# Sums of weight blocks in a seven-product scheme: formed by accumulating transfers instead of VectorE additions

## The chip, the cores and the metric

The kernel runs on one core of a Trainium2 chip. The metric is the device time of one execution in microseconds. Before the change, three runs gave 1434.34 us in the median (1432.75 to 1437.7).

The engines are called as the profile calls them: PE is the matrix engine (PEld its weight loads), DVE the vector engine, ACT the scalar engine, POOL the GpSimd engine and SP the sync engine, which here only issues transfers. A "transfer" is a DMA. SP, ACT and POOL each have a queue of their own in which their instructions, transfers included, are started in order.

## The reference

One decoder layer for a prompt of 1024 rows and 8 sample rows, all in float32 (`NT` = 1032 columns when the activations are stored transposed). After a normalisation, one projection `h @ w_in` (1024 to about 10,000 columns) feeds two branches; the change touches the weights of branch A's projection and of branch B's output projection:

```
proj = h @ w_in
hA, cA, bA, zA, qkv, zB, beta_raw, alpha_raw, gA, gB = jnp.split(proj, offs, axis=-1)
a_conv, new_buf_a = causal_dwconv(cA * hA, buf_a, conv_a_w)
yA = ((bA * a_conv) * jax.nn.silu(zA)) @ w_out_a
...                       # branch B: gated delta rule, o
yB = o.reshape(bsz, L, D_V).astype(x.dtype) @ w_out_b
merged = jax.nn.sigmoid(gA) * yA + jax.nn.sigmoid(gB) * yB
post = rmsnorm(merged @ w_o, norm_post)
```

Eight outputs are returned (both groups' rows and six new states). Only the products named above matter here.

## The kernel before, in words

**Precision.** Every large product is made of three matmuls of a reduced-precision type: an operand is split into a high part (`hi`, a rounding copy) and a low part (`lo`, the operand minus `hi`), and hi*hi, hi*lo and lo*hi are added in PSUM. So each block of weights costs one cast on ACT (`whi`) and one subtraction on DVE (`wlo`) before PE can use it.

**Stages.** A start, then a long run of ordinary projections (`run(jobs, 1, isp)`), then `products()`, `products_b()`, the output projection of branch A and the tail. The change lies in `products()` and `products_b()`.

**Seven products for eight.** There, output and operands are cut in two by two blocks and a Winograd form of Strassen's scheme is used: seven block products, called `P1, P2, P6, P7, P4, P5, P3` in the order of work. `products()` does this for five groups of column tiles (`t` = 3 to 7, called groups 3 to 7 below), `products_b()` for branch B's output projection with two halves `g` per product (group B). One product of one group is a *unit*: 48 matmuls of 258 columns. The weights of a group are four raw blocks of 128 x 1024 floats, `a11`, `a12`, `a21`, `a22` (keys `(group, odd, half, g)`), and the products use these: P1 a11; P2 a12; P6 a21 + a22 - a11; P7 a11 - a21; P4 a22; P5 a21 + a22 (`wsum`); P3 a12 - (a21 + a22 - a11). `evacuate` adds each product from PSUM to the output tiles (`acc`, or `mrg` in group B) on DVE; P1 is copied by ACT.

**How weights are prepared.** `weight_load` issues the raw blocks on SP's queue, two transfers of 256 KB a block. `weight_gen` waits until the unit before has begun (`unit[0] >= n - 1`), casts `whi` on ACT and subtracts `wlo` on DVE. The tiles `whi` and `wlo` have two buffers each, so the cast for a unit also waits until PE has finished the unit before the last. When P2's weights are split, four DVE additions of 128 x 1024 form the sums in place: `wsum`, then a21 (for P7), a11 (for P6) and a12 (for P3).

**What sets the order.** The generators (`weight_gen`, `park_gen`, `yblock_gen` and so on) are strands that a planner (`Sched`, `slot`, `force`) steps between groups of matmuls by assumed costs. The layer below places the recorded instructions into each engine's queue and may move them ahead of others; so the order in a queue is not that of the code, and it is shown below where it matters. Each engine works its queue in order: an instruction that waits holds up all behind it. Slots for raw blocks come from a common pool (`T4`).

**Other work in the same stretch.** `finish_group` closes a group on ACT and DVE, `park_gen` transforms the right operand of group B and stores it (`txs`), and `yblock_gen` loads it back: from `yBsc` on SP (`yraw`) for P1, P2, P3 and from `txs` on POOL's queue (`thi`, `tlo`) for the others. These 16 loads are all that POOL's queue issues before the change in these stages.

Lines: all calls go through one recording helper, so the profile has line L121 for nearly everything and the tiles' names tell the place: `wr` is a raw block, `wsum` the sum for P5, `pm_t` and `pa_t` are PSUM tiles.

Of the kernel before, what the change touches and what calls it, by code (L numbers as in the profile page):

```python
# [11 lines left out]
AF = mybir.ActivationFunctionType  # L12
ALU = mybir.AluOpType
# [3 lines left out]
P = 128  # L17
D = 1024
# [135 lines left out]
def hybrid_step(  # L154
# [9 lines left out]
    V, A, PE, GP, SY = (Paced(e, n, sched) for e, n in (  # L164
        (nc.vector, "V"), (nc.scalar, "A"), (nc.tensor, "PE"), (nc.gpsimd, "GP"), (nc.sync, "SY")))
# [12 lines left out]
    def tt(out, a, b, op):  # L178
        V.tensor_tensor(out=out, in0=a, in1=b, op=op)
# [15 lines left out]
    def act(out, in_, func, **kw):  # L195
        A.activation(out=out, in_=in_, func=func, **kw)
# [468 lines left out]
    def when(*conds):  # L665
        while not all(c() for c in conds):
            yield
# [710 lines left out]
    ACOL = (COL_H, COL_C, COL_B, COL_Z)  # L1378

    def alloc(key, side):  # L1380
        pools[key] = tc.alloc_tile_pool(name=key, bufs=1, side=side)
        return pools[key]

    UNITS = [(t, p, 0) for t in range(SG, NK) for p in PROD] + [("B", p, g) for p in PROD for g in range(2)]

    def weight_load(raw):
        for key in list(range(SG, NK)) + ["B"]:
            w, n = (w_out_b, 2) if key == "B" else (w_in, 1)
            for odd, half in ((0, 0), (0, 1), (1, 0), (1, 1)):
                for g in range(n):  # L1390
                    yield from when(lambda: len(raw) < 4 * n, lambda: T4.ready())
                    v = T4.get("wr", D)
                    for q in range(2):
                        c0 = (4 * g + 2 * q + odd) * P if n == 2 else ACOL[2 * q + odd] + key * P
                        SY.dma_start(out=v[:, q * 512:(q + 1) * 512].rearrange("p (k c) -> p k c", c=P),
                                     in_=w[0, half * 512:(half + 1) * 512, c0:c0 + P]
                                     .rearrange("(k p) c -> p k c", p=P))
                    raw[key, odd, half, g] = v
                    yield

    def weight_gen(raw):

        sums = {}
        for n, (key, p, g) in enumerate(UNITS):
            a11, a12, a21, a22 = ((key, o, hf, g) for o in range(2) for hf in range(2))
            src = {"P1": a11, "P2": a12, "P6": a11, "P7": a21, "P4": a22, "P5": None, "P3": a12}[p]
            yield from when(lambda: unit[0] >= n - 1, lambda: src is None or src in raw)
            hi_ = wpool.tile([P, NK, P], F32R, tag="whi", name="whi", bufs=2)
            lo_ = wpool.tile([P, NK, P], F32R, tag="wlo", name="wlo", bufs=2)
            hi, lo = (v.rearrange("p k c -> p (k c)") for v in (hi_, lo_))  # L1410
            v = raw[src] if src else sums.pop(g)
            A.copy(out=hi, in_=v)
            yield
            tt(lo, v, hi.bitcast(F32), ALU.subtract)
            made[key, p, g] = (hi_, lo_)
            yield
            if p == "P2":
                yield from when(lambda: a22 in raw and a21 in raw)
                s_ = wpool.tile([P, NK, P], F32, tag="wraw", name="wsum", bufs=3)
                s_ = sums[g] = s_.rearrange("p k c -> p (k c)")  # L1420
                tt(s_, raw[a21], raw[a22], ALU.add)
                yield
                tt(raw[a21], raw[a11], raw[a21], ALU.subtract)
                tt(raw[a11], s_, raw[a11], ALU.subtract)
                yield
                tt(raw[a12], raw[a12], raw[a11], ALU.subtract)
            elif p in ("P6", "P7", "P4", "P3"):
                T4.give(raw.pop(src))

    def park_gen():  # L1430

        for k in range(4):
            yield from when(lambda: T4.ready(2))
            a, b = T4.get("pa_", NT), T4.get("pb_", NT)
            SY.dma_start(out=a, in_=yBsc[k])
            SY.dma_start(out=b, in_=yBsc[4 + k])
            yield
            a1, a2, b1, b2 = a[:, 0:HT], a[:, HT:NT], b[:, 0:HT], b[:, HT:NT]
            tt(a1, a2, a1, ALU.subtract)
            tt(a2, b2, a2, ALU.subtract)  # L1440
            yield
            tt(b2, b2, a1, ALU.subtract)
            tt(b1, b1, b2, ALU.subtract)
            yield
            for r, v in enumerate((a, b)):
                yield from when(lambda: T4.ready(2))
                hi, lo = T4.get("phi", NT), T4.get("plo", NT)
                A.copy(out=hi.bitcast(F32R), in_=v)
                yield
                tt(lo.bitcast(F32R), v, hi, ALU.subtract)  # L1450
                T4.give(v)
                store(txs[r, 0, k].bitcast(F32), hi)
                store(txs[r, 1, k].bitcast(F32), lo)
                T4.give(hi)
                T4.give(lo)
                yield
        parked.append(True)
# [146 lines left out]
    def evacuate(p, v, ta, tb, half):  # L1604
        c1, c2 = (slice(o + half * PW, o + half * PW + PW) for o in (0, HT))
        C11, C12, C21, C22 = ta[:, c1], ta[:, c2], tb[:, c1], tb[:, c2]
        if p == "P1":
            A.copy(out=C11, in_=v)
            A.copy(out=C12, in_=v)
        for out, in_ in {"P1": (), "P2": ((C11, C11),), "P6": ((C12, C12),), "P7": ((C22, C12),),  # L1610
                         "P4": ((C21, C22),), "P5": ((C22, C22), (C12, C12)), "P3": ((C12, C12),)}[p]:
            tt(out, v, in_, ALU.add)

    gated = {}

# [52 lines left out]
    def to_products():  # L1668
        drain_bg()
        bp.release()  # L1670
        T4.extend(alloc("m", "left"), "sl", NSL, NT)
        raw = {}
        for g in (weight_load(raw), weight_gen(raw), block_gen()):
            start(g)
# [77 lines left out]
    T4 = Slots(alloc("t4", "left"), "t4", NT4, CY)  # L1752
# [64 lines left out]
    for j in range(9):  # L1817
        i, n, xr, mh, ml, held = pre.pop(j)
# [33 lines left out]
        for half in range(2):  # L1852
            hs = slice(half * 512, (half + 1) * 512)
            stt(yt[:n, hs], yt[:n, hs], r, xr[:n, hs], ALU.mult, ALU.add)
            out = y_prompt[0, i * P:(i + 1) * P, hs] if i < 8 else y_sample[:, 0, hs]
# [38 lines left out]
```

## Time and profile before

| | before |
|---|---|
| median of 3 runs | 1434.34 us |
| the profiled execution | 1434.01 us, span 1432.3 us |
| PE busy | 1401.0 us (98%) |
| DVE busy | 984.4 us (69%) |
| ACT busy | 656.4 us (46%) |
| POOL busy | 35.6 us (2%) |
| bytes moved by transfers | 158.59 MB, of these 8.46 MB from POOL's queue |
| granted PE clock | 0.998 |

The span runs from the first to the last instruction; the execution's own time is 1.7 us more. Matmuls are pipelined, so PE's busy time overlaps itself: one matmul of 258 columns has a mean of 282 ns in the records, but they start 120 ns apart. Times inside the span are given in us from its start. Group 3 begins at about 941, group 7's first product at 1103.33, group B at about 1143.6, and the seven-product stages end at about 1225.

### The profile page before, as it was taken

To read this page: it belongs to the slowest core of one execution; us is meant where nothing else is said; L and a number is where in the kernel's file an instruction comes from. 1 tells how busy PE (TensorE), PEld (TensorE's weight loads), DVE (VectorE), ACT (ScalarE), POOL (GpSimd) and SP (SyncE) were. 2 spreads that over 40 slices of the span, in tenths; PEclk is the share of its full clock that TensorE was granted. 3 is DMA by queue.
4 is the path that set the end of the run, shared out by engine and by line. 5 is a ranking of instruction groups with operands and counts; after the bars stand their busy time and mean duration, and the time that the engine had idled before them with its cause. 6 is when DMAs were issued, how large, how long until landed. Compare 5 with 4: busy or idle time off the path is not lost.

```text
span 1432.3 us, 25802 instructions
## 1 busy us (share of the span) xinstructions
PE 1401.0 (98%) x10130; PEld 1340.5 (94%) x10130; DVE 984.4 (69%) x2436; ACT 656.4 (46%) x1521; POOL 35.6 (2%) x59
## 2 busy tenths in 40 slices
PE   6999999899999999999999999999999999999997
PEld 4899999899999999999999999999999999999786
DVE  6754867759569585496864924988877867854553
ACT  6766453855528554466383332253323344532211
POOL 0000000100001000000000000000000110000000
PEclk9999999999999999999999999999999999999999
DMA  9523143132422324224132221344711885743221
GB/s 320 144 48 102 54 127 81 54 80 78 119 60 69 94 62 117 50 66 121 54 97 68 79 68 32 118 170 164 243 53 42 236 265 172 244 150 91 92 87 59
DMA packets 181922, 158.59 MB, mean 111 GB/s; under 512 B 25351, under 2 KB 157856, under 8 KB 181794
## 3 DMA queue, kind: packets, MB, share of 16 engines
q1 hardware_dynamic: 177248, 148.43, 35.2%
q0 software_dynamic: 4352, 8.46, 2.0%
q8 instruction: 79, 1.29, 0.4%
q14 instruction: 41, 0.34, 0.1%
q10 hardware_dynamic: 202, 0.08, 0.0%
HBM read 120.25 MB, written 36.91 MB: 110 GB/s over the span
## 4 chain that ended last, share of the span: by engine, by line
PE 84%; DVE 8%; DMA 5%; ACT 1%; issue 1%; SPq 1%; DVEq 0%; ACTq 0%
PE pm_t L121 63%; PE pa_t L121 19%; PE pb L121 2%; DVE acc L121 2%; DVE wlo L121 1%; DMA xs<-in_x_prompt_dram 1%; SPq L121 1%; DMA yraw<-yAsc 1%; DVE Tt L121 1%; DVE kq L121 1%; DMA wor<-in_w_o_dram 1%; DVE Ttmp L121 1%; DVE wr L121 0%; DMA yraw<-yBsc 0%; DMA pa__11678<-yBsc 0%
## 5 line engine op out<-in xcount | busy, mean ns | idle before, releaser
L121 PE MATMUL pm_t<-xh,whi 128*128 128x344 f32 (+1 forms) x1576 | 517.9, 329 | 2.2 <-ACT gate L121 2.2
L121 PE MATMUL pm_t<-xh,wlo 128*128 128x344 f32 (+1 forms) x1576 | 500.4, 318 | 0.0
L121 PE MATMUL pm_t<-xl,whi 128*128 128x344 f32 (+1 forms) x1576 | 500.1, 317 | 0.0
L121 PEld LDWEIGHTS pm_t<-xh,whi 128*128 128x128 f32 x1576 | 297.4, 189 | 4.7 <-ACT gate L121 2.5
L121 PEld LDWEIGHTS pm_t<-xl,whi 128*128 128x128 f32 x1576 | 297.3, 189 | 0.2
L121 PEld LDWEIGHTS pm_t<-xh,wlo 128*128 128x128 f32 x1576 | 296.9, 188 | 0.4
L121 DVE TENSOR_TENSOR wlo<-wraw,whi 128x512 fp32r<-128x512 f32 x136 | 91.8, 684 | 65.2 <-ACT whi L121 63.1
L121 ACT CAST whi<-wraw 128x512 fp32r<-128x512 f32 x136 | 82.7, 623 | 85.6 <-PE pm_t L121 83.6
L121 DVE TENSOR_TENSOR Ttmp<-Tt 32x30 f32<-32x30 f32 (+14 forms) x240 | 76.1, 317 | 14.7 <-DMA Tt<-sA 10.3
L121 DVE TENSOR_TENSOR Tt<-Tt,Ttmp 32x30 f32<-32x30 f32 (+14 forms) x240 | 76.2, 317 | 4.4
L121 ACT CAST whi<-wr 128x1024 fp32r<-128x1024 f32 x42 | 44.0, 1047 | 73.5 <-PE pa_t L121 34.9
L121 DVE SCALAR_TENSOR_TENSOR kq<-raw,vecs,kq 128x528 f32<-128x528 f32 x96 | 69.9, 758 | 1.5 <-ACT kq L121 1.3
L121 PE MATMUL pm_t<-thi,wlo 128*128 128x258 f32 x240 | 67.6, 283 | 1.6 <-DVE wlo L121 1.6
L121 PE MATMUL pm_t<-tlo,whi 128*128 128x258 f32 x240 | 67.6, 282 | 0.0
L121 PE MATMUL pm_t<-thi,whi 128*128 128x258 f32 x240 | 67.6, 282 | 0.0
L121 PE MATMUL pa_t<-thi,whi 128*128 128x258 f32 x224 | 63.3, 282 | 1.1 <-ACT whi L121 1.1
L121 PE MATMUL pa_t<-thi,wlo 128*128 128x258 f32 x224 | 63.4, 283 | 0.8 <-DVE wlo L121 0.8
L121 PE MATMUL pa_t<-tlo,whi 128*128 128x258 f32 x224 | 63.2, 282 | 0.0
L121 PE MATMUL pm_t<-yhi,whi 128*128 128x344 f32 x192 | 61.5, 321 | 0.0
L121 PE MATMUL pm_t<-ylo,whi 128*128 128x344 f32 x192 | 61.4, 321 | 0.0
L121 PE MATMUL pm_t<-yhi,wlo 128*128 128x344 f32 x192 | 61.4, 320 | 0.0
L121 DVE TENSOR_TENSOR wlo<-wr,whi 128x1024 fp32r<-128x1024 f32 x42 | 51.3, 1221 | 8.9 <-ACT whi L121 8.7
(406 smaller groups left out, 2834.0 us busy)
## 6 DMA issues: line engine op xcount, KB each, us to landing
wraw<-in_w_in_dram SPq DMA_DIRECT2D x60, 512.0 KB
wr<-in_w_in_dram SPq DMA_DIRECT2D x40, 256.0 KB
aw<-in_ada_w_dram SPq DMA_DIRECT2D x16, 512.0 KB
gBsc<-gate SPq DMA_DIRECT2D x8, 516.0 KB
gAsc<-gate SPq DMA_DIRECT2D x8, 516.0 KB
txs<-phi SPq DMA_DIRECT2D x8, 516.0 KB
txs<-plo SPq DMA_DIRECT2D x8, 516.0 KB
tlo<-txs POOLq DMA_DIRECT2D x8, 516.0 KB, 7.3
```

What stands on the lines that cost most here:

```text
L121: r = f(*args, **kw)
```

## The change

The four DVE additions of each group (and each half of group B) go. Transfers that add to what lies in the destination take their place; they are issued on POOL's queue (`GP.dma_start(..., accum_op=ALU.add)`), and their sign comes from ACT, which writes the negative of a block.

After P1's split: ACT writes -a11 into a new slot (the later a21) and then negates a11 in place. Then a21 and a22 are read from DRAM again and added to the slot of a11 (giving a21 + a22 - a11 for P6), and a21 is added to the new slot (a21 - a11 for P7). After P2's split: ACT negates a12 in place, a transfer inside SBUF adds a11's slot to it (for P3, with the sign turned), and `wsum` is loaded with a22 from SP's queue and a21 added to it. The block a21 is no longer loaded as such. P7 and P3 now have the opposite sign, so `evacuate` subtracts them.

```diff
--- before.py
+++ after.py
@@ -1383,18 +1383,27 @@
 
     UNITS = [(t, p, 0) for t in range(SG, NK) for p in PROD] + [("B", p, g) for p in PROD for g in range(2)]
 
+    def wd(v, key, add=False):
+
+        t, odd, half, g = key
+        w, n = (w_out_b, 2) if t == "B" else (w_in, 1)
+        for q in range(2):
+            c0 = (4 * g + 2 * q + odd) * P if n == 2 else ACOL[2 * q + odd] + t * P
+            out = v[:, q * 512:(q + 1) * 512].rearrange("p (k c) -> p k c", c=P)
+            in_ = w[0, half * 512:(half + 1) * 512, c0:c0 + P].rearrange("(k p) c -> p k c", p=P)
+            if add:
+                GP.dma_start(out=out, in_=in_, accum_op=ALU.add)
+            else:
+                SY.dma_start(out=out, in_=in_)
+
     def weight_load(raw):
         for key in list(range(SG, NK)) + ["B"]:
-            w, n = (w_out_b, 2) if key == "B" else (w_in, 1)
-            for odd, half in ((0, 0), (0, 1), (1, 0), (1, 1)):
+            n = 2 if key == "B" else 1
+            for odd, half in ((0, 0), (0, 1), (1, 1)):
                 for g in range(n):
                     yield from when(lambda: len(raw) < 4 * n, lambda: T4.ready())
                     v = T4.get("wr", D)
-                    for q in range(2):
-                        c0 = (4 * g + 2 * q + odd) * P if n == 2 else ACOL[2 * q + odd] + key * P
-                        SY.dma_start(out=v[:, q * 512:(q + 1) * 512].rearrange("p (k c) -> p k c", c=P),
-                                     in_=w[0, half * 512:(half + 1) * 512, c0:c0 + P]
-                                     .rearrange("(k p) c -> p k c", p=P))
+                    wd(v, (key, odd, half, g))
                     raw[key, odd, half, g] = v
                     yield
 
@@ -1414,18 +1423,26 @@
             tt(lo, v, hi.bitcast(F32), ALU.subtract)
             made[key, p, g] = (hi_, lo_)
             yield
-            if p == "P2":
-                yield from when(lambda: a22 in raw and a21 in raw)
+            if p == "P1":
+
+                yield from when(lambda: T4.ready())
+                raw[a21] = T4.get("wr", D)
+                act(raw[a21], raw[a11], AF.Copy, scale=-1.0)
+                act(raw[a11], raw[a11], AF.Copy, scale=-1.0)
+                wd(raw[a11], a21, True)
+                wd(raw[a11], a22, True)
+                wd(raw[a21], a21, True)
+            elif p == "P2":
+
+                act(raw[a12], raw[a12], AF.Copy, scale=-1.0)
+                GP.dma_start(out=raw[a12], in_=raw[a11], accum_op=ALU.add)
                 s_ = wpool.tile([P, NK, P], F32, tag="wraw", name="wsum", bufs=3)
                 s_ = sums[g] = s_.rearrange("p k c -> p (k c)")
-                tt(s_, raw[a21], raw[a22], ALU.add)
-                yield
-                tt(raw[a21], raw[a11], raw[a21], ALU.subtract)
-                tt(raw[a11], s_, raw[a11], ALU.subtract)
-                yield
-                tt(raw[a12], raw[a12], raw[a11], ALU.subtract)
-            elif p in ("P6", "P7", "P4", "P3"):
+                wd(s_, a22)
+                wd(s_, a21, True)
+            if p in ("P6", "P7", "P4", "P3"):
                 T4.give(raw.pop(src))
+            yield
 
     def park_gen():
 
@@ -1609,7 +1626,10 @@
             A.copy(out=C12, in_=v)
         for out, in_ in {"P1": (), "P2": ((C11, C11),), "P6": ((C12, C12),), "P7": ((C22, C12),),
                          "P4": ((C21, C22),), "P5": ((C22, C22), (C12, C12)), "P3": ((C12, C12),)}[p]:
-            tt(out, v, in_, ALU.add)
+            if p in ("P7", "P3"):
+                tt(out, in_, v, ALU.subtract)
+            else:
+                tt(out, v, in_, ALU.add)
 
     gated = {}
```

For one group this makes, before: 8 transfers of 256 KB from SP. After: 8 transfers of 256 KB from SP (six for a11, a12, a22, two for `wsum`), and from POOL eight accumulating transfers of 256 KB and one of 512 KB. Group B has this twice.

**The order on ACT around the last group of `products()`.** This is group 7, from its P1 to its P4. Before, `wr_12445` is a11, `wr_12531` a12, `wr_12587` a21 and `wr_12650` a22, `acc_12712` and `acc_12714` are tiles that P1 is copied to:

```order
L121 CAST whi_12656<-wr_12445 128x1024
L121 ACTIVATE acc_12279<-acc_12279 128x1032
L121 ACTIVATE acc_12276<-acc_12277,vecs2_83 128x1032
L121 CAST whi_12719<-wr_12531 128x1024
L121 COPY acc_12712<-pm_t_10869 128x258 x2
L121 COPY acc_12712<-pm_t_10870 128x258 x2
L121 COPY acc_12714<-pm_t_10871 128x258 x2
L121 CAST whi_12827<-wr_12445 128x1024
L121 COPY acc_12714<-pm_t_10872 128x258 x2
L121 CAST thi_12857<-yraw_12856 128x1032
L121 CAST whi_12885<-wr_12587 128x1024
L121 CAST thi_12947<-yraw_12946 128x1032
```

Now, with a11 in `wr_12213`, a12 in `wr_12504`, a21 in `wr_12721` and a22 in `wr_12537`:

```order
L121 CAST whi_12694<-wr_12213 128x1024
L121 ACTIVATE acc_12312<-acc_12312 128x1032
L121 ACTIVATE wr_12213<-wr_12213 128x1024
L121 ACTIVATE acc_12309<-acc_12310,vecs2_83 128x1032
L121 CAST whi_12831<-wr_12504 128x1024
L121 COPY acc_12756<-pm_t_10878 128x258 x2
L121 COPY acc_12756<-pm_t_10879 128x258 x2
L121 ACTIVATE wr_12504<-wr_12504 128x1024
L121 COPY acc_12758<-pm_t_10880 128x258 x2
L121 CAST whi_12894<-wr_12213 128x1024
L121 COPY acc_12758<-pm_t_10881 128x258 x2
L121 CAST thi_12902<-yraw_12901 128x1032
```

The negation of a11 stands two places behind P1's cast, and that of a12 among the copies of P1. The cast for P6 (`whi_12894`) keeps its place, but what it reads now comes from transfers. The write of -a11 into `wr_12721` has been moved far ahead, to before the casts for the group before's P4, P5 and P3.

**The order on POOL's queue for the same group.** Before, this queue has none of this work. Now:

```order
L121 DMA wr_12063<-wr_11772 128x1024
L121 DMA wr_12721<-in_w_in_dram 128x4x128 x2
L121 DMA wsum_13474<-in_w_out_b_dram 128x4x128 x2
L121 DMA wr_12213<-in_w_in_dram 128x4x128 x4
L121 DMA wr_12504<-wr_12213 128x1024
L121 DMA thi_13367<-txs_112 128x2x516
```

The first row is the sum for P3 of group 6; then come a21 for P7, a `wsum` that group B will use, the four additions to a11 for P6 (two halves of a21, then two of a22 on the same bytes) and the sum for P3 of group 7. Behind them stand the loads of group B's operand.

**The order on SP's queue** where the operand of group B (`yraw`) and the last weights (`wr_...` from `w_out_b`) are loaded. Before:

```order
L121 DMA yraw_12856<-yBsc_111 128x2x516
L121 DMA yAsc_110<-acc_12276 128x1032
L121 DMA wr_12894<-in_w_out_b_dram 128x4x128 x2
L121 DMA wr_13045<-in_w_out_b_dram 128x4x128
L121 DMA yraw_12946<-yBsc_111 128x2x516
L121 DMA wr_13045<-in_w_out_b_dram 128x4x128
L121 DMA yraw_13037<-yBsc_111 128x2x516
```

Now:

```order
L121 DMA yraw_12901<-yBsc_111 128x2x516
L121 DMA yAsc_110<-acc_12309 128x1032
L121 DMA wr_12924<-in_w_out_b_dram 128x4x128 x2
L121 DMA yraw_12976<-yBsc_111 128x2x516
L121 DMA yraw_13054<-yBsc_111 128x2x516
```

The second `yraw` load still follows a load of a block into a slot of the common pool, but `wr_12924` goes into the slot of group 7's a11, and waits until the sum for P3 (`wr_12504<-wr_12213`) has read it.

## The prediction

> **What bounds the kernel now.** I read first the page's list of engines, then the stretches of the product stages, then PE's waits there.
>
> ```profile
> PE 1401.0 (98%) x10130; PEld 1340.5 (94%) x10130; DVE 984.4 (69%) x2436; ACT 656.4 (46%) x1521; POOL 35.6 (2%) x59
> ...
> core 0: us, PE busy (x) PEld busy (x) DVE busy (x) ACT busy (x) POOL busy (x), PEclk, DMA share, GB/s
> 981.40:1021.60 40.20, 40.06 (x335) 39.86 (x334) 34.62 (x58) 15.37 (x22) 0.00 (x0) 1.00 0.58 196
> 1021.60:1063.20 41.60, 40.41 (x338) 40.21 (x337) 34.12 (x55) 12.09 (x18) 0.00 (x0) 1.00 0.37 104
> 1063.20:1103.40 40.20, 40.20 (x338) 40.20 (x337) 29.87 (x50) 11.74 (x18) 0.00 (x0) 1.00 0.24 67
> 1103.40:1143.60 40.20, 40.20 (x338) 40.20 (x338) 33.48 (x52) 15.56 (x21) 3.69 (x5) 1.00 0.72 210
> 1143.60:1225.00 81.40, 79.08 (x654) 78.46 (x654) 60.39 (x95) 39.85 (x52) 7.89 (x11) 1.00 0.67 216
> ```
>
> Each of the first four stretches is one group, seven units. Undisturbed it takes 40.20 us with PE busy throughout, so a unit takes 5.74 us. DVE has 6 to 10 us to spare in each. What PE loses in these stages to any other engine is all in one answer, the waits of PE from 880 to 1240 us:
>
> ```profile
> engine line waited for: us in total, times, longest us
> PE pm_t L121 <- DVE wlo L121: 1.6, 2, 1.2
> PE pa_t L121 <- ACT whi L121: 1.1, 1, 1.1
> PE pa_t L121 <- DVE wlo L121: 0.8, 1, 0.8
> ```
>
> That is 3.5 us of 1434, 0.24%. Relieving DVE cannot win more than these 3.5 us in these stages. Only two of the waits have the removed additions before them in the chain of waits or fall where DVE was late by itself: the 1.2 in group 5 and the 0.4 at the start of group B's P6.
>
> ```profile
> 1029.16 1.22 DVE wr L121
> ...
> 1030.85 0.86 DVE wr L121
> ...
> 1034.98 0.39 PE L121 MATMUL pm_t<-thi,wlo 128*128 128x258 f32 x1 [1.19 <-DVE wlo L121]
> 1167.34 0.39 PE L121 MATMUL pm_t<-thi,wlo 128*128 128x258 f32 x1 [0.43 <-DVE wlo L121]
> ```
>
> The first two rows are pieces of the chain, the other two the places on PE.
>
> **What is removed.** The four additions of a group and the sums of both halves of group B, 28 instructions:
>
> ```profile
> L121 DVE TENSOR_TENSOR wr<-wr 128x1024 f32<-128x1024 f32 x14 | 17.1, 1219 | 0.0
> L121 DVE TENSOR_TENSOR wsum<-wr 128x1024 f32<-128x1024 f32 x7 | 8.5, 1221 | 4.9 <-DMA wr<-in_w_in_dram 3.2 <-DMA wr<-in_w_out_b_dram 1.7
> L121 DVE TENSOR_TENSOR wr<-wsum,wr 128x1024 f32<-128x1024 f32 x7 | 8.5, 1218 | 0.0
> ```
>
> 17.1 + 8.5 + 8.5 = 34.1 us of DVE's time, hidden under PE. On the path they are worth the 1.2 us of group 5 and perhaps the 0.4 us at the start of group B's P6 (the other part of the 1.6): a gain of 0 to 1.6 us. The subtractions in `evacuate` are as long as the additions were.
>
> **What is added on ACT.** Three negations for each of the seven sets of sums, 21 instructions of 128 x 1024. The nearest row is ACT's scaling of a tile of 128 x 1032:
>
> ```profile
> L121 ACT ACTIVATE acc<-acc 128x1032 f32<-128x1032 f32 x5 | 5.3, 1065 | 5.9 <-DVE acc L121 5.9
> ```
>
> 21 x 1.06 = 22 us, 3.2 us a group, where ACT is idle for 24 us of 40. Cost on the path: nothing, as long as they stand behind the cast that PE wants next; the order on ACT shows that they do. Without that cover each would cost 1.06 us.
>
> **What is added in transfers.** From POOL 63 issues (nine for each set of sums); SP issues as many as before. A set moves 16 x 256 KB from DRAM instead of 8 and 512 KB inside SBUF: 2.5 MB more, 17.5 MB in all. In a group with a DMA share of 0.24 to 0.58 that has room. What counts is one chain: the weights of P6. P1's split must be through, then a11 is negated, a21 added, a22 added on the same bytes, and only then can the cast for P6 start. In group 7 the rows of ACT, DVE and PE are these:
>
> ```profile
> 1097.64 1.05 ACT L121 CAST whi<-wr 128x1024 fp32r<-128x1024 f32 x1 [4.71 <-PE pm_t L121]
> 1098.73 1.23 DVE L121 TENSOR_TENSOR wlo<-wr,whi 128x1024 fp32r<-128x1024 f32 x1 [0.20 <-ACT whi L121]
> 1103.33 0.28 PE L121 MATMUL pm_t<-xh,whi 128*128 128x258 f32 x1
> 1109.20 1.05 ACT L121 CAST whi<-wr 128x1024 fp32r<-128x1024 f32 x1 [0.71 <-PE pm_t L121]
> 1114.81 0.28 PE L121 MATMUL pm_t<-thi,whi 128*128 128x258 f32 x1
> ```
>
> P1's `wlo` ends at 1099.96; the negation ends 1.06 later, at 1101.0. PE begins P6 at 1114.81, and cast and subtraction take 1.05 + 1.23, so the last good start of the cast is 1112.5. **The transfers have 11.5 us.** In it stand, one behind the other: a transfer that lands, one that waits for it and lands, and one issue (the second halves are issued one behind the first). No accumulating transfer is in the trace of before. Nearest are POOL's 16 loads of 516 KB:
>
> ```profile
> L121 POOL DMA_DIRECT2D thi<-txs x8: 713/720/746, 1133.1 to 1155.4; - x8
> ...
> DMA to landing us min/median/max: 4.1/8.0/10.4
> ```
>
> and SP's loads of raw blocks and operands, seen where someone waited for them:
>
> ```profile
> 1073.24 1.79 SPq L121 DMA_DIRECT2D wr<-in_w_in_dram  x2
> 1078.18 1.23 DVE L121 TENSOR_TENSOR wsum<-wr 128x1024 f32<-128x1024 f32 x1 [0.85 <-DMA wr<-in_w_in_dram]
> 1108.07 0.37 SPq L121 DMA_DIRECT2D yraw<-yBsc  x1
> 1111.87 1.06 ACT L121 CAST thi<-yraw 128x1032 fp32r<-128x1032 f32 x1 [1.07 <-DMA yraw<-yBsc]
> ```
>
> The second 256 KB was issued by 1075.0 and had landed at 1078.2: 3.1 us. The 516 KB took 3.8. An addition must read the 256 KB that come and the 256 KB that are there, as much as a load of 516 KB reads, so I take the lower end of POOL's rows, rounded up: 4.5 us from issue to landing; bounds 3.1 and 10.4. An issue took 0.72 for 256 pieces of 2 KB; a 256 KB block has 512 pieces, so 0.72 to 1.44. The chain is 2 x 4.5 + 0.7 to 1.4 = **9.7 to 10.4 us against 11.5**: in time, by about 1 us. It is late from 5.0 us a transfer on. At 3.1 it has 4 us to spare; at POOL's median of 8.0 it is late by 5.2 to 5.9. That median comes from a stretch with a DMA share of 0.96:
>
> ```profile
> 1000.00:1040.00 40.00, 38.68 (x321) 38.27 (x320) 35.64 (x57) 13.52 (x19) 0.00 (x0) 1.00 0.75 238
> 1120.00:1160.00 40.00, 40.00 (x336) 40.00 (x336) 35.02 (x50) 17.15 (x28) 10.86 (x15) 1.00 0.96 283
> ```
>
> Group 3 and group B have a longer lead (P1's first cast comes long before the stage; group B has two units a product), groups 4, 6 and 7 about the lead just worked out. Group 5 has least:
>
> ```profile
> 1015.61 1.04 ACT L121 CAST whi<-wr 128x1024 fp32r<-128x1024 f32 x1
> 1019.47 1.22 DVE L121 TENSOR_TENSOR wlo<-wr,whi 128x1024 fp32r<-128x1024 f32 x1
> 1032.92 0.28 PE L121 MATMUL pm_t<-thi,whi 128*128 128x258 f32 x1
> ```
>
> The negation can end at 1020.7 + 1.06 = 1021.8, the cast must start by 1032.92 - 2.3 = 1030.6: 8.8 us, where DMA is busy to 0.75. With 9.7 to 13 us it is 1 to 4 us late, where the old additions made it 1.2 late: I take 2.5.
>
> The Trainium skill ("DMA: Bandwidth & Descriptors", Bandwidth and Anatomy of one DMA) fits a transfer from GpSimd as 2.0 us plus the bytes at 436 GB/s; by this estimate 256 KB land in 2.6 us and the chain takes 6 us, in time even in group 5. The trace speaks against it: the same fit gives 3.2 us for 516 KB, and the quickest of POOL's took 4.1.
>
> **What else is behind it.** On ACT the last copies of P1 stand behind P6's cast, so a late cast also holds DVE's additions of P2; that costs no more than the same lateness. On SP the load of a `w_out_b` block waits for group 7's sum for P3, and `yraw` behind it: the sum is issued at about 1111, lands by 1116, `yraw` goes out at about 1118 instead of
>
> ```profile
> 1116.20 0.37 SPq L121 DMA_DIRECT2D yraw<-yBsc  x1
> 1120.61 1.06 ACT L121 CAST thi<-yraw 128x1032 fp32r<-128x1032 f32 x1 [4.32 <-DMA yraw<-yBsc]
> 1121.57 1.05 ACT L121 CAST whi<-wr 128x1024 fp32r<-128x1024 f32 x1
> ```
>
> and lands 4.4 later, at 1122.4; P4's cast behind it starts at 1123.4. P4 begins 4 units after 1103.33, at 1126.3, so 1124.0 would do: 0. In group B the extra traffic meets a DMA share of 0.96 and loads that ACT already waits for; I put 1 us there (0 to 5).
>
> **Sum**, on the profiled execution's 1434.01: DVE's waits -1.6, group 5 +2.5, groups 4, 6, 7 at 0, group B +1: +1.9, 1435.9. The median is 0.33 above that execution; rounded, **1436**.
>
> **Rivals.** (1) *The two additions in a row come too late* in groups 4 to 7: slower. Each transfer at 7 to 8.6 us makes a group 3.2 to 7 late, four groups 13 to 28 us: 1447 to 1462. It decides from 5.0 us a transfer, and beyond 0.3% from about 5.6. For it speaks POOL's median; against it, that this comes from the busiest stretch. (2) *Queues in order*: a `wsum` addition that waits for SP, or `yraw` and `txs` loads behind an addition that waits, hold up P4 of group 7 or group B by 2 to 4 us at two or three places: 1440 to 1444. For it speaks the order on SP and POOL; against it, a margin of 0.6 us or more at each place that I followed. (3) *DVE was dearer than it looks*: all 3.5 us come back and no transfer is late: 1430.5. Against it, the 0.8 and the 1.1 lie in group B, behind ACT, which waits for a load there. (4) *DVE holds up the issues*: each of the three issues in the chain waits for the end of a DVE instruction of 1.22 us, the chain is 3.7 longer and 2 to 2.6 late, four times: 1444. Against it, POOL's issues took 713 to 746 ns while DVE was busy for 35 of 40 us. This is the trap that the Trainium skill names ("SBUF — State Buffer", two separate sides): while DVE runs a two-port instruction, GpSimd cannot write descriptors. It says itself that the two-input additions were not seen to do so; the trace agrees, by those 713 to 746 ns. That the change is not what it says is excluded by the order: the 28 additions are gone and the accumulating transfers stand in POOL's queue.
>
> **How the numbers follow.** Two measurements of this kernel can be told apart from about 0.3%, 4.3 us. No measurable change (my forecast, 1431 to 1438): 0.47. Rival 1: 0.31. Rival 2: 0.14. Rival 4: 0.02. Rival 3: 0.06, with whatever makes it more than 0.3%. So slower 0.47, same 0.47, faster 0.06; the likeliest time is 1436. Cases of one sign hold nearly all the rest, so the range goes from 1430 (rival 3) to 1460 (rival 1 with transfers near 8.5 us).
>
> **What would show it.** Right: DVE about 950 us busy, ACT about 678, POOL with 63 issues more; additions of 256 KB landing in 4 to 5 us outside group B; PE waits for `whi` or `wlo` under 5 us in all from 880 to 1240. Wrong: landings above 6 us, or rows in which ACT's `whi` waits for a transfer into `wr` and PE for that `whi`, once a group (rival 1); ACT waiting for `yraw` or `sg` for longer than now (rival 2); POOL issues of 2 us and more (rival 4); a group in 40.2 us everywhere and a time under 1430 (rival 3).

## The result and the profile after

The changed kernel took **1570.66 us** (median of four executions, 1568.39 to 1574.02) against 1434.75 us before (median of four): 1.0947 times as long, with a 95% interval from 1.092 to 1.0975. It is slower by 136 us, far outside the range of the prediction.

The rows of the page of the changed kernel that answer to those shown of before are the busy times, the clock by slices of 39 us, and POOL's own DMA queue:

```profile
PE 1417.7 (90%) x10130; PEld 1354.8 (86%) x10130; DVE 955.8 (61%) x2408; ACT 677.7 (43%) x1542; POOL 114.9 (7%) x122
PEclk9999999999999999999999996977888977999999
q0 software_dynamic: 34928, 26.81, 11.2%
```

DVE, ACT and the 63 additional issues are what the change said. PE is busy for 16.7 us longer with the same 10130 matmuls, and in eight of the slices from the 25th to the 34th it has less than nine tenths of its clock, which it had in every slice before the change. The waits of PE in the changed kernel's product stages, 880 to 1400 us:

```profile
engine line waited for: us in total, times, longest us
PE pa_t L121 <- ACT whi L121: 53.2, 3, 25.3
PE pm_t L121 <- ACT whi L121: 43.4, 3, 23.6
PE pm_t L121 <- issue: 24.0, 1, 24.0
```

These seven waits are 120.6 us. With the 16.7 us of longer matmuls they account for the loss of 136. Each is a wait for the cast of P6's weights: 24.0 us in group 3, 16.6, 23.6, 11.2 and 8.7 in groups 4 to 7, 11.1 and 25.3 in the two halves of group B. On ACT of the changed kernel, the casts for P6 in groups 3, 4 and 5 and the negation of a11 in group 4 are:

```profile
975.16 1.04 ACT L121 CAST whi<-wr 128x1024 fp32r<-128x1024 f32 x1 [29.30 <-DMA wr<-in_w_in_dram]
...
1006.81 1.06 ACT L121 ACTIVATE wr<-wr 128x1024 f32<-128x1024 f32 x1 [0.39 <-DVE wlo L121]
...
1036.28 1.04 ACT L121 CAST whi<-wr 128x1024 fp32r<-128x1024 f32 x1 [19.46 <-DMA wr<-in_w_in_dram]
...
1102.55 1.04 ACT L121 CAST whi<-wr 128x1024 fp32r<-128x1024 f32 x1 [28.05 <-DMA wr<-in_w_in_dram]
```

From one cast for P6 to the next it is 61.1 and 66.3 us, where a group took 40.2 before. In group 4 the negation ends at 1007.87 and the cast starts at 1036.28: 28.4 us, for which the prediction had 9.7 to 10.4. What lies between is seen in POOL's row of instructions for the same group (start, duration, and in brackets the idle time before it):

```profile
991.91 1.30 POOL L121 DMA_DIRECT2D wr<-in_w_in_dram  x1 [15.27 <-ACT wr L121]
997.56 1.30 POOL L121 DMA_DIRECT2D wr<-in_w_in_dram  x1 [4.36 <-issue]
1002.53 1.29 POOL L121 DMA_DIRECT2D wsum<-in_w_in_dram  x1 [3.67 <-DVE acc L121]
1007.72 1.30 POOL L121 DMA_DIRECT2D wsum<-in_w_in_dram  x1 [3.90 <-issue]
1012.66 1.29 POOL L121 DMA_DIRECT2D wr<-in_w_in_dram  x1 [3.64 <-ACT whi L121]
1017.89 1.30 POOL L121 DMA_DIRECT2D wr<-in_w_in_dram  x1 [3.94 <-issue]
1026.41 1.29 POOL L121 DMA_DIRECT2D wr<-in_w_in_dram  x1 [7.22 <-issue]
1031.49 1.30 POOL L121 DMA_DIRECT2D wr<-in_w_in_dram  x1 [3.79 <-issue]
1036.85 0.90 POOL L121 DMA_DIRECT2D wr<-wr  x1 [4.06 <-DMA wr<-in_w_in_dram]
```

The first pair is a21's block, the second a `wsum`, the next four are the additions to a11. An issue takes 1.30 us, but the next starts 3.6 to 4.4 us after it and once 7.2, also where the two write to different halves and wait for nothing of each other ("issue"). By the landings in the trace, each of the seven issues after the first of these rows, up to the last of a11's, starts 0.3 us after the one before it has landed. The distance from start to start, mostly 5 us, is that from issue to landing, in the list of the changed kernel's transfers (KB each, median us to landing):

```profile
wr<-in_w_in_dram POOLq DMA_DIRECT2D x30, 256.0 KB, 4.7
wsum<-in_w_in_dram POOLq DMA_DIRECT2D x10, 256.0 KB, 4.8
```

So the transfers go one at a time, and nine for a set take some 45 us of a group of 40. The 28.4 us of group 4 have two parts: 4.8 us until the `wsum` pair ahead is out of the way and a11's first addition is issued, and 23.6 us for a11's own four, one landing after the other. In groups 3 to 7 the four took 19.5 to 23.6 us each time; the wait ahead of them, from the end of a11's negation, was 22.3, 4.8, 16.9, 0.8 and 1.3 us. That was not in the prediction, nor in any of its rivals.

The longer matmuls are those behind a long wait. On PE of the changed kernel, P6 of group 4 begins so:

```profile
1037.38 0.58 PE L121 MATMUL pa_t<-thi,whi 128*128 128x258 f32 x1 [16.63 <-ACT whi L121]
...
1040.95 0.42 PE L121 MATMUL pa_t<-thi,whi 128*128 128x258 f32 x1
1041.17 0.33 PE L121 MATMUL pa_t<-tlo,whi 128*128 128x258 f32 x1
1041.33 0.28 PE L121 MATMUL pa_t<-thi,wlo 128*128 128x258 f32 x1
1041.45 0.28 PE L121 MATMUL pa_t<-thi,whi 128*128 128x258 f32 x1
```

For 3.8 us the matmuls start 0.21 us apart, then 0.12, and the granted clock is 0.50 at first. This wait costs some 1.7 us more than itself. Behind the other six the slow stretch lasts 4.0 to 7.0 us; worked out from the starts, the seven together make about 16 of the 16.7 us. The Trainium skill ("TensorE: Matmul & The Clock Gate", Part 1) states half the clock for about 3.4 us after an idle window; the clock of 0.50 agrees, but the stretch was longer here, 3.8 to 7.0 us.

### The profile page after: what moved, and what is told of

It is laid out like the page before. It is cut to its first block, busy times and chain, and to the rows that moved or that the text cites. A ratio compares the mean times of both kernels' runs of the same rounds, so it can differ in the third digit from the quotient of the medians.

```text
span 1568.5 us, 25952 instructions
## 1 busy us (share of the span) xinstructions
PE 1417.7 (90%) x10130; PEld 1354.8 (86%) x10130; DVE 955.8 (61%) x2408; ACT 677.7 (43%) x1542; POOL 114.9 (7%) x122
## 3 DMA queue, kind: packets, MB, share of 16 engines
q0 software_dynamic: 34928, 26.81, 11.2%
## 5 line engine op out<-in xcount | busy, mean ns | idle before, releaser
L121 PE MATMUL pm_t<-thi,whi 128*128 128x258 f32 x240 | 72.4, 302 | 67.3 <-ACT whi L121 43.4
L121 PEld LDWEIGHTS pm_t<-thi,whi 128*128 128x128 f32 x240 | 49.3, 205 | 68.1 <-ACT whi L121 44.0
L121 PEld LDWEIGHTS pa_t<-thi,whi 128*128 128x128 f32 x224 | 44.9, 200 | 53.8 <-ACT whi L121 53.8
L121 PE MATMUL pm_t<-thi,wlo 128*128 128x258 f32 x240 | 71.8, 299 | 1.8 <-DVE wlo L121 1.8
L121 PE MATMUL pm_t<-tlo,whi 128*128 128x258 f32 x240 | 71.4, 298 | 0.0
L121 POOL COPY raw<-hist_q 128x24 f32<-128x24 f32 x24 | 19.3, 804 | 637.6 <-DVE ro_a L121 255.6
```

Source lines behind the costliest of these rows:

```text
L121: r = f(*args, **kw)
```

## The experiments

Each edit is against the changed kernel unless it says otherwise; `...` stands for lines that are not shown, and what stands behind # is a note of this document. A time without an interval is a single execution. "Theory R" and "theory A" were the first two: that POOL's queue has no room for the descriptors of a second adding transfer, or that adding transfers are taken one at a time as such.

**More room for descriptors.** The kernels set aside `DYN` = 2048 bytes of each partition for the descriptors that POOL writes.

```diff
-DYN = 2048
+DYN = 8192
-NAW = 8
+NAW = 6
...
-        raw = wpool.tile([P, NK, P], F32, tag="wraw", name="wraw", bufs=3)
+        raw = wpool.tile([P, NK, P], F32, tag="wraw", name="wraw", bufs=2)
...
-                s_ = wpool.tile([P, NK, P], F32, tag="wraw", name="wsum", bufs=3)
+                s_ = wpool.tile([P, NK, P], F32, tag="wraw", name="wsum", bufs=2)
```

> The changed kernel with four times the space in which POOL's queue builds its descriptors (8192 instead of 2048 bytes of a partition); to make room, two buffers fewer for the start-up's weights and two instead of three for the raw weights and wsum. Theory R (the space holds one accumulating transfer of 512 pieces; the next issue waits for room): issues of independent accumulating transfers follow each other by about 1.3 us, ACT's cast for P6 waits no more than 10 us in all in groups 4 to 7, and the time falls to 1435 to 1450 us. Theory A (accumulating transfers of one queue go one at a time, each after the landing of the one before): the issues stay 4.7 to 5.2 us apart and the time stays at 1560 to 1580 us.

Measured: 1479.09 us, 1.0311 times before (1.028 to 1.0342), 92 us less than the change. The issues go out in pairs, two in 2.6 us, and theory A falls. But 43 us stay, so that theory R's time is missed too, and PE still waits 30.0 us for casts of weights, more than theory R allowed. The control has the same fewer buffers at 2048 bytes:

> The control for the larger space: the same fewer buffers, with 2048 bytes as in the change. Both theories: issues 4.7 to 5.2 us apart, 1560 to 1585 us; what it differs from 1570.66 is the cost of the fewer buffers.

Measured: 1577.41 us, as expected; by this one execution the fewer buffers cost 7 us.

**The same transfers without adding.** `accum_op=ALU.add` is left out of all 63.

> The changed kernel with the same 63 transfers on POOL's queue, of the same pieces and to the same places, that only write and do not add (the sums of weights are left out). Theory R (room for the pieces): nothing changes, issues 4 to 5 us apart, 1550 to 1575 us. Theory A (it is the adding that goes one at a time): issues of independent transfers about 1.3 us apart, landing in 3 to 4 us, 1434 to 1450 us.

Measured: 1449.62 us; the sums are missing in it. POOL's row, with a11's two pairs in group 4 and, from 1026.23, a `wsum` pair and a11's first two transfers in group 5:

```profile
982.21 1.49 POOL L121 DMA_DIRECT2D wr<-in_w_in_dram  x2 [4.85 <-ACT wr L121]
986.00 1.50 POOL L121 DMA_DIRECT2D wr<-in_w_in_dram  x2 [2.31 <-DMA wr<-in_w_in_dram]
...
1026.23 1.50 POOL L121 DMA_DIRECT2D wsum<-in_w_in_dram  x2 [12.77 <-DVE acc L121]
1027.72 0.75 POOL L121 DMA_DIRECT2D wr<-in_w_in_dram  x1
1030.32 0.75 POOL L121 DMA_DIRECT2D wr<-in_w_in_dram  x1 [1.85 <-issue]
```

In group 4 two of 512 pieces go out back to back, 0.75 us each (1.30 with adding), and only the second pair waits for the first to land. In group 5 three go out in a row, and the fourth only 0.3 us after the first has landed: 2048 bytes have room for 1536 pieces that only write, and not for 2048. By itself the time speaks for theory A, which the larger room had refuted: both hold together if a piece that adds takes more of the room than one that writes. The next run shows that it takes twice as much. The Trainium skill ("Collectives: The Full Stack", Part 3) says that the addition of a collective takes two read descriptors for a chunk where a copy takes one. The factor of two in the room agrees with that, and so, roughly, do the issue times, 1.30 against 0.75. The number of descriptors itself is in no trace here. What the traces do count is packets: POOL's queue moves the same 26.81 MB in 34928 of them with adding and in 9840 without.

**The same additions in smaller transfers**, at 2048 bytes:

```diff
-                GP.dma_start(out=out, in_=in_, accum_op=ALU.add)
+                for k in range(0, 4, 2):
+                    GP.dma_start(out=out[:, k:k + 2], in_=in_[:, k:k + 2], accum_op=ALU.add)
```

> The changed kernel with each accumulating transfer of 512 pieces cut into two of 256 (the half along k), so 8 become 16 for each set of sums. Theory R: two or more of 256 pieces fit and go out 0.7 us apart, so the rate by bytes is no lower: 1500 to 1575 us. Theory A: each still waits for the landing of the one before, about 3.5 to 4 us each, 16 of them 56 to 64 us a group instead of 40: 1640 to 1700 us.

Measured: 1513.33 us, 57 us less with twice as many transfers from DRAM. POOL's row shows why:

```profile
909.50 3.85 POOL L121 DMA_DIRECT2D wr<-in_w_in_dram  x3 [189.62 <-DMA wr<-in_w_in_dram]
916.44 1.22 POOL L121 DMA_DIRECT2D wr<-in_w_in_dram  x1 [3.09 <-issue]
```

Three of 256 pieces go out in a row and the fourth waits: 768 pieces that add have room in 2048 bytes, 1024 have not, half of what there is for pieces that only write. Further on up to six stand in one row, but by their landings no more than three were ever under way. That adding transfers are not taken one at a time as such is settled by these rows.

**How much room is enough.** 4096 bytes, with one start-up buffer fewer (`NAW` = 7):

> The change with 4096 bytes for the descriptors (and one buffer fewer for the start-up's weights). Theory R, if an accumulating transfer of 512 pieces needs more than half of 2048 bytes: at least two fit, issues go out in pairs about 1.3 us apart, with a wait before a third; between 1571 and 1479 us, nearer to 1479: 1480 to 1510 us. Theory A': the gain at 8192 came from something else that differs there (order, buffers): 1560 us or more.

Measured: 1482.35 us. On POOL, group 4's a11 and, from 1036.22, a `wsum` and a11 of group 5:

```profile
986.54 2.60 POOL L121 DMA_DIRECT2D wr<-in_w_in_dram  x2 [2.79 <-ACT wr L121]
991.96 1.28 POOL L121 DMA_DIRECT2D wr<-in_w_in_dram  x1 [2.82 <-DMA wr<-in_w_in_dram]
994.00 1.30 POOL L121 DMA_DIRECT2D wr<-in_w_in_dram  x1 [0.75 <-DMA wr<-in_w_in_dram]
1001.25 0.90 POOL L121 DMA_DIRECT2D wr<-wr  x1 [5.95 <-DMA wr<-in_w_in_dram]
...
1036.22 2.61 POOL L121 DMA_DIRECT2D wsum<-in_w_in_dram  x2 [12.17 <-DVE acc L121]
1037.72 2.43 POOL L121 DMA_DIRECT2D wr<-in_w_in_dram  x1
1041.61 1.28 POOL L121 DMA_DIRECT2D wr<-in_w_in_dram  x1 [1.46 <-issue]
```

Three of 512 pieces fit, twice the 768 that fit in half the bytes. What is left in the same kernel is, first, waits of PE from 880 to 1300 us:

```profile
PE pa_t L121 <- ACT whi L121: 17.0, 3, 12.3
PE pm_t L121 <- ACT whi L121: 13.2, 2, 11.4
```

and, in its list of transfers, a later landing where two are under way:

```profile
wr<-in_w_in_dram POOLq DMA_DIRECT2D x30, 256.0 KB, 6.3
```

From the first of a11's issues in group 4 to `wr<-wr`, which waits for the last landing, it is 14.7 us (986.54 to 1001.25), where the prediction had 11.5 to give. In group 5 a `wsum` pair that waited 12.2 us stands ahead of a11's: a11's negation had ended at 1031.95, 5.8 us before its first addition went out. By group the waits are 2.6, 11.4, 2.0 and 1.8 us (groups 4 to 7) and 12.3 (group B). The first place is rival 1 of the prediction, the second the queue of its rival 2, though not where that rival saw it.

**Transfers left out.** "Theory Q" is from here on that the loss comes from the transfers that stand one behind the other in POOL's queue. First all of them are left out, and the sums with them:

> The change without any of the adding transfers (the sums of weights are left out, wsum holds a22 alone): the 28 additions are gone from DVE, the 21 negations stand on ACT. Theory Q and the prediction's terms for DVE and ACT: nothing is late, 1430 to 1436 us, PE waits from 880 to 1240 us under 4 us. Rival: the negations hold up casts, 1.06 us each, 5 to 20 us in all: 1440 to 1455 us.

Measured: 1429.38 us, 0.9958 times before (0.9945 to 0.9971). Its waits of PE from 880 to 1300 us are

```profile
PE pm_t L121 <- DVE wlo L121: 0.3, 1, 0.3
PE pa_t L121 <- DVE wlo L121: 0.3, 1, 0.3
```

So the negations cost nothing that PE waits for, and with them DVE's relief is worth 6.4 us by the medians, 4 to 8 by the interval. The trace accounts for 2.9 of them (3.5 of waits less 0.6); where the others come from is not settled. Then only wsum's two are left out:

> The change without the two transfers that add a21 to wsum (P5's weights are a22 alone). Theory Q: a group's round (61 us from P6's cast to the next) loses the two that stand ahead of a11's in the queue, 10 us; five groups, 40 to 50 us less: 1520 to 1530 us. Rival L (only the landings of a11's own transfers count; wsum is off the path): 1560 to 1571 us.

Measured: 1541.15 us, 30 less. Its casts for P6 in groups 3 to 5 start at 963.07, 1018.26 and 1074.25, 55 to 56 us apart instead of 61 to 66. What stands ahead in the queue counts, as theory Q has it, though at 6 us a group and not 8 to 10, so that its time is missed.

**a21's sum behind a11's:**

```diff
-                act(raw[a21], raw[a11], AF.Copy, scale=-1.0)     # at P1
...
-                wd(raw[a21], a21, True)
...
+                act(raw[a21], raw[a11], AF.Copy, scale=-1.0)     # at P2, from the finished a11
+                wd(raw[a21], a22, True)
```

> The change with a21's sum taken from the finished a11 (the block is -(a11's sum), then a22 is added from DRAM in two transfers; P7's sign turns back), so that these two stand behind a11's four in the queue instead of ahead. Same number of transfers. Theory Q: P6's weights come 10 us earlier, P7's later; the nine transfers still take 45 us of a group of 40, so 5 to 15 us a group stay: 1465 to 1520 us. Rival L: 1555 to 1575 us.

Measured: 1578.28 us, not faster, outside both ranges. It does not test the order cleanly, since the turning of a21's block, which now waits for a11's transfers, stands on ACT ahead of casts:

```profile
1107.16 1.06 ACT L121 ACTIVATE wr<-wr 128x1024 f32<-128x1024 f32 x1 [27.26 <-DMA wr<-in_w_in_dram]
```

ACT stood still for 27.3 us there. The run shows something else in POOL's row:

```profile
970.50 1.30 POOL L121 DMA_DIRECT2D wr<-in_w_in_dram  x1 [4.84 <-issue]
971.26 1.47 POOL L121 DMA_DIRECT2D wr<-wr  x1
```

An adding transfer of 128 pieces goes out right behind one of 512 that has not landed: the pieces count, not the adding.

**All sums from SBUF, 128 pieces each**, at 2048 bytes:

```diff
+                wd(s_, a21)                                        # at P1, by SP
+                GP.dma_start(out=s_, in_=raw[a22], accum_op=ALU.add)
...
                 act(raw[a11], raw[a11], AF.Copy, scale=-1.0)
-                wd(raw[a11], a21, True)
-                wd(raw[a11], a22, True)
+                GP.dma_start(out=raw[a11], in_=s_, accum_op=ALU.add)
...
+                act(raw[a21], raw[a11], AF.Copy, scale=-1.0)       # at P2
+                GP.dma_start(out=raw[a21], in_=raw[a22], accum_op=ALU.add)
```

> The same sums, still added by POOL's transfers on signs that ACT turns, at 2048 bytes, but each from a block that is in SBUF already (128 pieces of 4 KB): wsum is a21 as SP loads it, plus a22's block; a11 becomes -a11 + wsum in one transfer; a21's block is -(that) + a22's block (P7's sign turns back); a12 as in the change. Four transfers a set instead of nine, 28 instead of 63. Theory Q (the loss comes from the number and the pieces of the transfers that stand one behind the other in POOL's queue): from a11's negation to P6's cast there is one transfer, 0.9 us of issue and 4.6 to land, 5.5 us of the 11.5 that there are; a group has 18 to 22 us of transfers; no wait for P6 in groups 4 to 7, 1432 to 1440 us. Theory T (any accumulating transfer before P6 is too late, because the negation itself comes late or queues behind other things): ACT's cast for P6 waits 5 us or more once a group, 1455 us or more.

Measured: 1451.44 us, 1.0106 times before (1.0083 to 1.013). 119 us of the 136 are gone without more room. The rest has two places. One is in its groups of lines (behind the bars: busy time and mean ns, then idle time before and for what):

```profile
L121 ACT ACTIVATE wr<-wr 128x1024 f32<-128x1024 f32 x21 | 22.5, 1069 | 32.6 <-DMA wr<-wsum 28.0 <-DVE wlo L121 4.6
```

The other is on POOL:

```profile
1030.67 0.86 POOL L121 DMA_DIRECT2D wsum<-wr  x1 [13.37 <-DMA wsum<-in_w_in_dram]
1031.33 1.08 POOL L121 DMA_DIRECT2D wr<-wsum  x1
```

ACT waits 28 us for transfers in order to turn a21's block, with casts behind it; and a `wsum` that waits for SP's load stands ahead of group 5's a11.

**Mixed versions.** Loads and wsum as before the change, three sums by transfers from SBUF (`mix1`); P6's sum on DVE too (`mix2`); `mix1` in groups 3 to 7 with group B wholly on DVE (`mix3`).

```diff
+                tt(s_, raw[a21], raw[a22], ALU.add)                # mix1, mix2, at P1
...
+                GP.dma_start(out=raw[a11], in_=s_, accum_op=ALU.add)   # mix1, on -a11
+                tt(raw[a11], s_, raw[a11], ALU.subtract)           # mix2 instead
```

> All four raw blocks are loaded by SP as before the change, and DVE forms wsum (7 of its 28 additions). The other three sums are transfers from SBUF, one each, at 2048 bytes: a11 becomes -a11 + wsum, a21's block -(that) + a22 (turned by ACT behind P6's cast), a12 becomes -a12 + a11's sum. 21 transfers. Against the version with all sums from SBUF it takes wsum out of POOL's queue (there one that waited 13.4 us for SP's load stood ahead of a11's) and ACT's turning of a21's block from ahead of the casts (there ACT waited 28.0 us for transfers into a11's block). Theory Q: nothing is late, PE waits from 880 to 1240 us under 5 us, three quarters of what leaving out all additions wins (6.4 us): 1430 to 1434 us. Theory T (a transfer before P6 is late whatever stands in the queue): as with all from SBUF, 1445 to 1455 us.

> As the run before it, but DVE forms a11's sum for P6 too (14 of its 28 additions); ACT turns a21's block and a12, and two transfers a set, from SBUF, add to them (P7, P3). Theory Q: no transfer stands before P6, half of the 6.4 us: 1431 to 1435 us. Theory T: the same, since no transfer stands before P6; it falls with P7 late, 1440 us or more.

> As the first of the two mixed versions (DVE forms wsum, the other three sums by one transfer each from SBUF) in groups 3 to 7; in group B DVE forms all four sums, as before the change. Theory G (a transfer from SBUF before P6 is in time where DMA is not full, as in groups 5 to 7 there, which took 40.0 us of 40; what was lost, 11.7 us of PE time from 1120 to 1200, is group B's, where DMA's share was 1.03): the time from 1120 to 1240 comes back, 1433 to 1438 us. Theory T (a transfer before P6 costs wherever it stands): 1444 us or more.

Measured: 1451.80 us (1.011, 1.0089 to 1.0132), 1440.00 us (1.0023, 1.001 to 1.0035) and 1445.38 us (1.006, 1.0038 to 1.0082). The first two were to be faster than before by theory Q, and were not. Why `mix2`, with no transfer before P6, is not faster is not settled; PE waits 7.4 us in it from 880 to 1300, against 3.5 before. `mix1` came out at theory T's number, but not for theory T's reason: three stretches of it (PE busy in the second column, its clock and the DMA share towards the end) are

```profile
1040.00:1080.00 40.00, 40.00 (x337) 40.00 (x336) 26.69 (x46) 14.53 (x20) 2.57 (x3) 1.00 0.44 106
1080.00:1120.00 40.00, 40.00 (x337) 40.00 (x336) 25.47 (x45) 14.51 (x20) 2.57 (x3) 1.00 0.33 85
...
1160.00:1200.00 40.00, 32.38 (x237) 31.46 (x237) 15.26 (x25) 18.78 (x29) 10.35 (x13) 0.89 1.03 286
```

Where DMA is a third to a half busy, a transfer before P6 costs nothing; in group B, at a share of 1.03, 7.6 us of 40 were lost. `mix3` gave back 6.4 us of the 15 over before, so group B is not all: of the rest PE waits 3.3 us between 1120 and 1160 and 4.7 from 940 to 1040, nearly all for DVE's `wlo`, and no run here tells what moved it.

**Room for two, and one transfer before P6.** With 4096 bytes:

```diff
                 act(raw[a11], raw[a11], AF.Copy, scale=-1.0)
-                wd(raw[a11], a21, True)
-                wd(raw[a11], a22, True)
+                wd(s_, a22)                                        # wsum, moved here from P2
+                wd(s_, a21, True)
+                GP.dma_start(out=raw[a11], in_=s_, accum_op=ALU.add)
                 wd(raw[a21], a21, True)
```

> The change with 4096 bytes for the descriptors, and P6's sum formed in one transfer (-a11 + wsum, from SBUF) instead of two pairs from DRAM, one pair behind the other; wsum and a21's sums come from DRAM as in the change. 42 transfers. Theory C (what 4096 bytes leave, 48 us over the kernel before, is the chain of two landings of 6 us and their issues before P6, as the first rival of the prediction has it): P6's cast waits no more than 1 us a group, 1438 to 1455 us. Theory H (it is the additions to wsum and to a21's block that stand ahead of a11's in the queue and wait for loads): the waits for P6 stay, 1465 us or more.

Measured: 1437.00 us, against 1482.35 with two pairs before P6. Theory C holds, its time 1 us under the range: the stretches are full except in group B, where the one wait for P6 is 4.8 us:

```profile
1000.00:1040.00 40.00, 40.00 (x336) 40.00 (x336) 29.63 (x50) 17.56 (x24) 9.64 (x8) 1.00 1.06 251
1040.00:1080.00 40.00, 40.00 (x336) 40.00 (x336) 25.65 (x44) 13.55 (x20) 4.37 (x4) 1.00 0.59 134
...
1160.00:1200.00 40.00, 34.74 (x271) 34.23 (x270) 18.93 (x31) 13.96 (x14) 2.37 (x3) 0.91 0.70 210
```

The edit takes away the second landing and three of the nine transfers of a set at once; what each is worth is not told apart. The same with 2048 bytes tells whether the room is still needed:

> P6's sum in one transfer as in the run with 4096 bytes, at 2048 bytes, in groups and group B alike. Theory R with C: the pairs for a21's block and for wsum that stand ahead of a11's transfer go one at a time, 20 us and its own 6 against 11.5: P6 10 to 15 us late a group, 1480 to 1510 us. If the chain of two landings were all that counts, it would be as with 4096 bytes: 1435 to 1445 us.

Measured: 1465.24 us, 28 more. Both are needed, though the lack of room costs less than the 43 to 73 us expected.

**The version that is faster than both**: as `ring4096_one`, with group B's four sums on DVE as before the change, and its control, the kernel before with the same room and buffers.

```diff
+            if p == "P2" and key == "B":
...
+                tt(s_, raw[a21], raw[a22], ALU.add)
...
+                tt(raw[a21], raw[a21], raw[a11], ALU.subtract)
+                tt(raw[a11], s_, raw[a11], ALU.subtract)
...
+                tt(raw[a12], raw[a11], raw[a12], ALU.subtract)
+            elif p == "P1" and key != "B":
```

> 4096 bytes for the descriptors and P6's sum in one transfer from wsum, as in the run before, in groups 3 to 7; in group B DVE forms the four sums as before the change. Theory C: groups 4 to 7 take 40.0 us of 40 as there (against 38.7 from 1000 to 1040 before), group B's wait of 4.8 us for the cast of weights and the lower clock behind it go: 1429 to 1434 us, faster than before by 0.2 to 0.5%. Rival (the gain is used up by traffic in group B, or by the start-up with a buffer fewer): 1435 to 1442 us.

> The control for it: the kernel before the change, with 4096 bytes for the descriptors and one buffer fewer for the start-up's weights. Both theories: as before, 1433 to 1440 us.

Measured: 1431.25 us, 0.9961 times before (0.9948 to 0.9973), and 1436.60 us for the control (1.0, 0.999 to 1.0011). From 880 to 1240 us its only wait of PE is

```profile
PE pa_t L121 <- DVE wlo L121: 0.3, 1, 0.3
```

## Why the prediction was wrong

**The bound** was read rightly: PE, with 3.5 us of waits to win and any lateness of P6's weights paid in full. With all transfers left out 2.9 of the 3.5 came back.

**The step that failed** is the price of an issue in the chain for P6: "one issue (the second halves are issued one behind the first)", 0.7 to 1.4 us. The issue itself took 1.30, inside the bounds. But a second one did not follow: with 2048 bytes it waited until the one before had landed, 3.6 to 4.4 us and once 7.2 in group 4. The bounds came from POOL's loads of 256 pieces, which do go out 0.7 us apart; that pieces that add, and twice as many, could fill the queue's room was not asked. It counts everywhere: a11's four transfers are four landings and not two, 19.5 to 23.6 us in groups 3 to 7 where 9.7 to 10.4 were forecast. The pairs for a21 and `wsum`, which the order showed ahead of them and which were costed at nothing, are four landings more; of these a11's had to wait for 4.8 us in group 4, 16.9 in group 5 and 22.3 in group 3. So the chain was 28.4 us long in group 4, and group 3, which was to have a longer lead and no cost, lost 24.0. More room, with nothing else to gain from it, gave 88 to 92 of the 136 us back.

**The landing** was sized rightly for what the change does, 4.5 taken and 4.7 measured, but with no other of POOL's transfers under way. With room for several it is 6.1 to 6.3, over the 5.0 from which the prediction itself called the chain late, and then **rival 1** is what happens in groups 4, 6 and 7 of the run with 4096 bytes, at 1.8 to 2.6 us each. P6's sum in one transfer instead of two pairs took the time there from 1482 to 1437, but that also ended the larger waits of group 5 and took most of group B's away. At 2048 bytes its sign came true (ACT's `whi` waits for `wr` once a group) without its cause (landings above 6).

**Rival 2**, an addition that waits at the head of the queue, is in group 5 of the run with 4096 bytes, a `wsum` ahead of a11's that waited 12 us and held a11's for 5.8 of them; the prediction looked for it at group 7's P4 and in group B. **Rival 4** did not occur: every issue of an addition took 0.9 to 1.5 us.

**DVE's relief** was taken at 1.6 and is larger: 2.9 by the trace, 6.4 by the medians. **The negations** at 0 were right. **Group B** at 1 us (0 to 5) was too little: in the changed kernel PE waits 36.4 us there; with room and one transfer before P6 it waits 4.8 us and loses clock behind it; with the sums on DVE it does not.

So the forecast of no change had a term missing and not only a wrong size, and none of the rivals held it; the chance of 0.47 for "slower" was right by its sign alone.

## What to carry to other kernels

Before transfers that add are put on POOL's queue one behind the other, count their pieces against the bytes set aside for descriptors (`DYN`), each piece that adds for two that only write: where the second has no room, the price of an issue is a whole landing, and everything ahead in the queue is paid in landings too. In a chain that a matmul waits for, form the sum in one transfer from a block that is already in SBUF, with long pieces, and leave such transfers out of a stretch where DMA is full. What the trace of before shows of one kind of transfer is a bound for another only if pieces, adding and room are alike.

## What the runs showed of the hardware

2048 bytes held 768 pieces of adding transfers but not 1024 (three of 256 in a row, one of 512); 4096 bytes held three of 512. Of transfers that only write, 2048 bytes held three of 512 pieces but not four. An issue of 512 pieces took 1.30 us with adding and 0.75 without; one of 128 pieces 0.90 and 0.55. Adding 256 KB from DRAM into a raw block landed 4.7 us after its issue in the median with no other of POOL's under way, and 6.1 to 6.3 with room for several. A PE idle of 16.6 us was followed by 3.8 us of matmuls at 0.21 us instead of 0.12; behind one of 24.0 us it was 7.0 us.
